# Gate and up by seven half-size products on TensorE, the gated product kept in DRAM, and the down product as a phase of its own

## The chip, the cores and the metric

The kernel runs on one core of one Trainium2 chip (trn2). The metric is the device time of one execution in microseconds; lower is better. All data are 32-bit floats in DRAM. The program is written in Bass and Tile: the program text gives operations and tiles, and a planner puts the instructions of each engine in a fixed order before the launch.

## The reference, cut to what matters

```python
SEQ, D_MODEL, D_FF, DEPTH = 512, 2048, 5632, 1
h = x                                              # 512 x 2048
xn = rms_norm(h, attn_norm_w)
...                                                # attention, convolution and recurrence groups
h = h + mix @ w_out
xn = rms_norm(h, ffn_norm_w)
ff = jax.nn.silu(xn @ w_gate) * (xn @ w_up)        # two products 512 x 2048 x 5632
h = h + ff @ w_down                                # 512 x 5632 x 2048
return rms_norm(h, final_norm_w)                   # y * rsqrt(mean(y*y) + 1e-6) * w
```

## The kernel before, in words

Activations lie transposed: a tile has 128 features on the partitions and the 512 tokens along the free axis, so `h` is 16 tiles of 128x512 and the gated product 44. Each float32 operand is split into a high part, rounded to float32r by a ScalarE copy, and a low part, the difference, by a VectorE subtraction (`split`, lines 130 to 138). A product of two such operands is three matmuls, high by high, high by low, low by high (`mm3`, lines 140 to 144). The weight is always the stationary operand (128x128), the activations the moving one.

Weights come from DRAM in half-blocks of 128x1024 (512 KB), each eight 128x128 stationary tiles. `weights` (lines 124 to 128) loads one through SyncE's DMA queue and splits it. It has two buffers for the loaded block (`raw`) and three each for the two parts (`wh`, `wl`). It runs under `high_priority(offset=6000)`: where the planner has several instructions of an engine that are ready, these come before all that stand up to 6000 places earlier in the program. The planner may also move matmuls past one another.

`cols_tile` (lines 146 to 155) makes one output tile of 128x512 in one PSUM bank: for a contraction of 16 tiles that is two half-blocks and, at three per contraction tile, 48 matmuls. `project` (660 to 675) makes `h` from `w_out`: per tile it loads `x`, adds the bank, splits `h * ffn_norm_w` into `hh` and `hl`, and adds up squares (ScalarE squares, GpSimd sums). `project_end` (677 to 680) makes `rstd`.

`ff_tile` (683 to 692) makes one of the 44 tiles of the gated product: 48 matmuls for gate, 48 for up, all 128 columns by 512 tokens; VectorE multiplies both banks by `rstd`, ScalarE applies silu, GpSimd multiplies the two, and the result is split for the next product. `ffn` (763 to 770) interleaves this with `down`: after each four tiles, `down` (694 to 701) adds their part of the down product to all 16 tiles of `h` in SBUF. The last four tiles go through `down_last` (703 to 757), which works by halves of the tokens (matmuls of 128x256), adds up the squares of the final `h`, and then makes the final norm and the output.

`run` (772 to 840) opens and closes the areas of SBUF and PSUM. Tiles of a new area may lie where tiles of a closed one lay; then their first writer waits for the last reader of what lay there. The gated product stays in SBUF, in the area `mix`.

Of the kernel before, what the change touches and what calls it, by code (L numbers as in the profile page):

```python
# [15 lines left out]
P = 128  # L16
# [11 lines left out]
GF = 4  # L28
NCHUNK = NF // GF
NB = S // P  # L30
# [41 lines left out]
class Area:  # L72
    """A pool whose tiles are named by a tag with its own number of buffers."""

# [15 lines left out]
class Trunk:  # L90
# [26 lines left out]

    # ---- weights: one half-block is [128, 1024] float32
    def weight_tiles(self):
# [19 lines left out]

    def mm3(self, out, a, b, first, last):  # L140
        mm = self.nc.tensor.matmul
        mm(out, a[0], b[0], start=first, stop=False)  # L142
        mm(out, a[0], b[1], start=False, stop=False)  # L143
        mm(out, a[1], b[0], start=False, stop=last)  # L144
# [70 lines left out]

    # ---- constants
    def consts(self):
# [103 lines left out]

    # ---- HGRN2, one head
    def hgrn_head(self, r2, w, hd):
# [106 lines left out]

    # ---- Conformer convolution
    def conv_tile(self, r1, gbank, abank, i):
# [36 lines left out]

    # ---- latents  # L470
    def latent(self, w, area, tag):
# [36 lines left out]

    # ---- attention
    def attention(self, w, r3):  # L510
# [147 lines left out]

    # ---- output projection and residual
    def project(self, w, r4):  # L660
        nc = self.nc
        self.hw = []
        sq_sum = self.sq_sum = r4("acc")
        for m in range(KT):
            nc.sync.dma_start(self.h[:, m], self.io["x"][m])
            bank = self.cols_tile(w, self.mix_y + self.mix)
            nc.vector.tensor_tensor(self.h[:, m], self.h[:, m], bank, op=ALU.add)
            self.hw.append(self.split(self.h[:, m], self.hp("hh", F32R), self.hp("hl", F32R),
                                      self.col("ffn_w", m)))
            if m == 0:  # L670
                nc.scalar.activation(sq_sum, self.h[:, m], AF.Square)
            else:
                q = r4("sq")
                nc.scalar.activation(q, self.h[:, m], AF.Square)
                nc.gpsimd.tensor_tensor(sq_sum, sq_sum, q, op=ALU.add)

    def project_end(self, r4):
        t = [r4(i) for i in ("sq", "sq", "acc")]
        r = self.rsqrt(self.sum_over_partitions(self.sq_sum), D, "eps", *t)
        self.nc.gpsimd.tensor_copy(self.rstd, r)  # L680

    # ---- feed-forward
    def ff_tile(self, w, r5):
        nc = self.nc
        gbank = self.cols_tile(w, self.hw)
        ubank = self.cols_tile(w, self.hw)
        g, u = r5("g"), r5("u")
        nc.vector.tensor_tensor(g, gbank, self.rstd, op=ALU.mult)  # L688
        self.last_silu = nc.scalar.activation(g, g, AF.Silu)
        nc.vector.tensor_tensor(u, ubank, self.rstd, op=ALU.mult)  # L690
        nc.gpsimd.tensor_tensor(u, u, g, op=ALU.mult)  # L691
        return self.split(u, self.mx("mx", F32R), self.mx("mx", F32R))

    def down(self, w, ff):
        nc = self.nc
        for m2 in range(KT // 2):
            h, l = self.weights(next(w))
            for i in range(2):
                m = 2 * m2 + i
                bank = self.four_tile(h, l, 4 * i, ff)  # L700
                nc.vector.tensor_tensor(self.h[:, m], self.h[:, m], bank, op=ALU.add)  # L701

    def down_last(self, w, ff, r5):
        """The last part of the product, the final norm and the output, by halves of the tokens."""
        nc = self.nc
        self.tables_after(self.last_silu)
        wt = []
        for m2 in range(KT // 2):
# [3 lines left out]
            else:  # L712
                raw = self.wp.tile([P, 1024], F32, tag="raw", name="raw", bufs=2)
                nc.sync.dma_start(raw, next(w))
                for s in (slice(0, S), slice(S, 2 * S)):
                    wt.append(self.split(raw[:, s], self.hp("hh", F32R), self.hp("hl", F32R)))
        n = S // 2
        acc = r5("acc")
        for th in range(2):
# [16 lines left out]
            for m in POOL_OUT:  # L736
                scaled[m] = o = self.mx("mx")
# [5 lines left out]
            r = self.rsqrt(bank, D, "eps", r5("g")[:, :n], r5("u")[:, :n], r5("sq", F32, (P, n)))  # L743
            for m in range(0, KT, 2):
                if m in scaled:
# [5 lines left out]
                    continue  # L751
                o = self.mx("mx")
                for i in range(2):
# [3 lines left out]
                self.put_out(m, ts, o)  # L757

    def put_out(self, m, ts, o):
# [3 lines left out]
    def ffn(self, wg, wd, r5):  # L763
        ff = [self.ff_tile(wg, r5) for _ in range(GF)]
        for c in range(NCHUNK - 1):
            nxt = [self.ff_tile(wg, r5)]
            self.down(wd, ff)
            nxt += [self.ff_tile(wg, r5) for _ in range(GF - 1)]
            ff = nxt
        self.down_last(wd, ff, r5)  # L770

    def run(self):
# [54 lines left out]
        ckvn.close()  # L827
        self.hp = area("hw", {"hh": KT, "hl": KT})
        late = area("late", {"h": 1}, "right")
        self.h = late("h", F32, (P, KT, S))  # L830
# [3 lines left out]
        self.ps = area("banks3", {"mm": 6, "ax": 2}, space=PSUM)  # L834
        self.project_end(r4)
        r4.close()
        r5 = area("ffn", {"g": 1, "u": 1, "sq": 3, "acc": 1}, "right")
        self.ffn(stream("w_gu"), stream("w_down"), r5)
        for a in (r5, late, self.hp, self.mx, self.ps):
# [21 lines left out]
def _arrange(inp):  # L861
# [36 lines left out]
    dn = a["w_down"][0]  # L898
    out["w_down"] = c(np.concatenate([_blocks_cols(dn[i * GF * P:(i + 1) * GF * P]) for i in range(NCHUNK)]))

# [54 lines left out]
```

## Time and profile before

| what | value |
|---|---|
| timed runs | 2212.8 us median of 3 (2211.44 to 2213.72) |
| profiled execution, first to last instruction (span) | 2210.9 us |
| TensorE matmul (PE) busy | 2175.6 us, 98% |
| TensorE weight load (PEld) busy | 1805.6 us, 82% |
| VectorE (DVE) busy | 1085.3 us, 49% |
| ScalarE (ACT) busy | 713.0 us, 32% |
| GpSimd (POOL) busy | 234.6 us, 11% |
| DMA | 220.52 MB, mean 100 GB/s |
| output projection, the matmuls after attention | up to 754.7 us of the span |
| gate, up and down, 512 tokens a matmul | 754.7 to 2148.1 us |
| last part of down, final norm, output | 2148.1 to 2210.9 us |

The only time that the profile gives for the execution is its span; the median of the timed runs is 1.9 us above it. Matmuls are pipelined: a record is longer than the distance to the next, so a rate is read as a stretch of time over the matmuls that began in it. "PEld" is the load of the stationary operand, which runs beside matmuls.

### The profile page before, as it was taken

To read this page: it belongs to the slowest core of one execution; us is meant where nothing else is said; L and a number is where in the kernel's file an instruction comes from. 1 tells how busy PE (TensorE), PEld (TensorE's weight loads), DVE (VectorE), ACT (ScalarE), POOL (GpSimd) and SP (SyncE) were. 2 spreads that over 40 slices of the span, in tenths; PEclk is the share of its full clock that TensorE was granted. 3 is DMA by queue.
4 is the path that set the end of the run, shared out by engine and by line. 5 is a ranking of instruction groups with operands and counts; after the bars stand their busy time and mean duration, and the time that the engine had idled before them with its cause. 6 is when DMAs were issued, how large, how long until landed. Compare 5 with 4: busy or idle time off the path is not lost.

```text
span 2210.9 us, 24879 instructions
## 1 busy us (share of the span) xinstructions
PE 2175.6 (98%) x10036; PEld 1805.6 (82%) x10036; DVE 1085.3 (49%) x1368; ACT 713.0 (32%) x1081; POOL 234.6 (11%) x195
## 2 busy tenths in 40 slices
PE   7999999999999999999999999999999999999997
PEld 6888788788778888888888888888888888888887
DVE  8896685557443334334343443434344343433437
ACT  6324664457432322222222222222222222222223
POOL 4102573100011100000000000000000000000001
PEclk9999999999999999999999999999999999999999
DMA  6233422313153333332323333333333332332332
GB/s 184 90 118 98 138 86 82 102 58 92 38 181 95 96 95 96 100 100 96 96 95 96 100 93 104 96 95 96 98 102 96 95 95 95 97 103 92 100 103 98
DMA packets 72595, 220.52 MB, mean 100 GB/s; under 512 B 7504, under 2 KB 15952, under 8 KB 72480
## 3 DMA queue, kind: packets, MB, share of 16 engines
q1 hardware_dynamic: 70192, 216.47, 31.4%
q10 hardware_dynamic: 2176, 2.10, 0.3%
q8 instruction: 79, 1.29, 0.2%
q0 software_dynamic: 112, 0.36, 0.0%
q14 instruction: 36, 0.29, 0.0%
HBM read 210.51 MB, written 8.39 MB: 99 GB/s over the span
## 4 chain that ended last, share of the span: by engine, by line
PE 94%; DVE 1%; ACT 1%; DMA 1%; POOL 1%; issue 1%; SPq 0%; DVEq 0%; ACTq 0%
PE mm L142 29%; PE mm L144 29%; PE mm L143 29%; PE lv L371 1%; PE ob L608 1%; PE lv L144 1%; PE lv L143 1%; PE lv L142 1%; DMA xraw<-in_x 1%; PE sc L583 0%; PE sc L584 0%; PE tb L600 0%; POOL ps L361 0%; DVE wl L134 0%; DMA raw<-in_w_down 0%
## 5 line engine op out<-in xcount | busy, mean ns | idle before, releaser
L133 ACT CAST wh<-raw 128x1024 fp32r<-128x1024 f32 (+1 forms) x379 | 391.3, 1034 | 1240.8 <-PE mm L143 1082.0
L134 DVE TENSOR_TENSOR wl<-raw,wh 128x1024 fp32r<-128x1024 f32 (+1 forms) x379 | 514.2, 1358 | 452.9 <-ACT wh L133 452.7
L142 PE MATMUL mm<-hh,wh 128*128 128x512 f32 x1408 | 548.1, 389 | 0.0
L144 PE MATMUL mm<-hh,wl 128*128 128x512 f32 x1408 | 547.7, 389 | 0.0
L143 PE MATMUL mm<-hl,wh 128*128 128x512 f32 x1408 | 547.7, 389 | 0.0
L142 PE MATMUL mm<-mx,wh 128*128 128x512 f32 (+1 forms) x944 | 361.4, 384 | 2.2 <-ACT mx L136 1.6
L144 PE MATMUL mm<-mx,wl 128*128 128x512 f32 (+1 forms) x944 | 362.3, 384 | 0.3 <-DVE wl L134 0.3
L143 PE MATMUL mm<-mx,wh 128*128 128x512 f32 (+1 forms) x944 | 362.3, 384 | 0.0
L143 PEld LDWEIGHTS mm<-hl,wh 128*128 128x128 f32 x1408 | 264.4, 188 | 55.1 <-issue 0.2
L142 PEld LDWEIGHTS mm<-hh,wh 128*128 128x128 f32 x1408 | 264.3, 188 | 55.0 <-issue 0.2
L144 PEld LDWEIGHTS mm<-hh,wl 128*128 128x128 f32 x1408 | 264.4, 188 | 54.8
L142 PEld LDWEIGHTS mm<-mx,wh 128*128 128x128 f32 x944 | 177.0, 188 | 37.6 <-ACT mx L136 2.0
L144 PEld LDWEIGHTS mm<-mx,wl 128*128 128x128 f32 x944 | 177.4, 188 | 35.8 <-DVE wl L134 1.2
L701 DVE TENSOR_TENSOR h<-h,mm 128x512 f32<-128x512 f32 x160 | 109.9, 687 | 196.9 <-PE mm L144 196.9
L143 PEld LDWEIGHTS mm<-mx,wh 128*128 128x128 f32 x944 | 177.4, 188 | 35.3 <-DVE mx L137 0.5
L691 POOL TENSOR_TENSOR u<-u,g 128x512 f32<-128x512 f32 x44 | 56.4, 1281 | 1327.5 <-ACT wh L133 1286.5
L142 PE MATMUL mm<-xh,wh 128*128 128x512 f32 x400 | 160.4, 401 | 6.8 <-ACT wh L133 6.8
L143 PE MATMUL mm<-xl,wh 128*128 128x512 f32 x400 | 158.6, 397 | 0.5 <-DVE xl L137 0.5
L144 PE MATMUL mm<-xh,wl 128*128 128x512 f32 x400 | 156.8, 395 | 0.0
L690 DVE TENSOR_TENSOR u<-mm,rstd 128x512 f32<-128x512 f32 x44 | 30.5, 692 | 145.5 <-PE mm L144 145.5
L688 DVE TENSOR_TENSOR g<-mm,rstd 128x512 f32<-128x512 f32 x44 | 30.4, 692 | 144.2 <-PE mm L144 144.2
L142 PEld LDWEIGHTS mm<-xh,wh 128*128 128x128 f32 x400 | 76.2, 191 | 23.6 <-ACT wh L133 6.0
(288 smaller groups left out, 1940.1 us busy)
## 6 DMA issues: line engine op xcount, KB each, us to landing
raw<-in_w_gu SPq DMA_DIRECT2D x176, 512.0 KB, 3.5
raw<-in_w_down SPq DMA_DIRECT2D x88, 512.0 KB, 3.5
raw<-in_w_cols SPq DMA_DIRECT2D x42, 512.0 KB, 3.5
raw<-in_w_out SPq DMA_DIRECT2D x32, 512.0 KB, 3.5
raw<-in_w_rows SPq DMA_DIRECT2D x16, 512.0 KB, 3.5
raw<-in_w_attn SPq DMA_DIRECT2D x14, 512.0 KB, 3.4
xraw<-in_x SPq DMA_DIRECT2D x16, 256.0 KB, 3.3
raw<-in_w_first SPq DMA_DIRECT2D x16, 256.0 KB, 3.2
```

What stands on the lines that cost most here:

```text
L133: nc.scalar.copy(h, src)
L134: nc.vector.tensor_tensor(l, src, h.bitcast(F32), op=ALU.subtract)
L142: mm(out, a[0], b[0], start=first, stop=False)
L143: mm(out, a[0], b[1], start=False, stop=False)
L144: mm(out, a[1], b[0], start=False, stop=last)
L371: nc.tensor.matmul(bank[:, c * 64:(c + 1) * 64], e[:, c * P:(c + 1) * P], ap_of(e, c * P + h, [2 * h, 64 // h], [1, h]), start=True, stop= ...
L608: nc.tensor.matmul(obank[:, qs], pt[:, js], vt[h // 4, j][:, hs], start=j == 0, stop=j == i)
L688: nc.vector.tensor_tensor(g, gbank, self.rstd, op=ALU.mult)
L690: nc.vector.tensor_tensor(u, ubank, self.rstd, op=ALU.mult)
L691: nc.gpsimd.tensor_tensor(u, u, g, op=ALU.mult)
L701: nc.vector.tensor_tensor(self.h[:, m], self.h[:, m], bank, op=ALU.add)
```

## The change

Gate and up are taken together, for 42 of the 44 tiles, as a product of a 2x2 block matrix of weights (the two halves of the contraction by gate and up) with a 2x2 block matrix of activations (the two halves of the contraction by the two halves of the tokens), in the form of Strassen and Winograd: seven products of half size, each 8 contraction tiles by 256 tokens, in place of eight. Two tiles (`PLAIN`) are made as before. The activations are not multiplied by `rstd` first; `h * ffn_norm_w` is kept as a float32 tile `hf`, from which `token_sums` makes the four sums of blocks that the algorithm needs, in two parts each. The sums of weight blocks are made per tile, in place in the loaded blocks.

The gated product is stored in a DRAM tile `ffd`, one tile of 256 KB each, and `h` in `hd`. A down phase of its own follows: it loads eight tiles of the gated product at a time through ScalarE's queue, splits them, and makes five passes over the 16 tiles of `h` with 24 matmuls each (128x512), then `down_last` with four tiles as before. The up branch is no longer multiplied by `rstd`; in place of that `h` is multiplied by `rms` (one over `rstd`) and the final norm's epsilon is scaled to match. Comments and docstrings were taken out. `mm3` passes a further keyword on to its matmuls.

```diff
+CF = 8
+NCHUNK = NF // CF
+PLAIN = 2
+HALF = 256
...
     def project(self, w, r4):
+            t = self.hf[:, m]
+            nc.sync.dma_start(t, self.io["x"][m])
             bank = self.cols_tile(w, self.mix_y + self.mix)
+            nc.vector.tensor_tensor(t, t, bank, op=ALU.add)
+            nc.scalar.dma_start(self.hd[m], t)
+            self.hw.append(self.split(t, self.hp("hh", F32R), self.hp("hl", F32R), self.col("ffn_w", m)))
...
+            nc.scalar.activation(t, t, AF.Copy, scale=self.col("ffn_w", m))
...
+    def token_sums(self, sp, tp):
+        n = KT // 2
+        H = {i: (sp("sh", F32R, (P, n, HALF)), sp("sl", F32R, (P, n, HALF))) for i in (1, 2, 3, 4)}
+        for j in range(0, n, 4):
+            q = lambda k, t: self.hf[:, k * n + j:k * n + j + 4, t * HALF:(t + 1) * HALF]
+            def parts(t, i):
+                self.split(t, *(x[:, j:j + 4] for x in H[i]))
+            s1 = tp("s", F32, (P, 4, HALF))
+            tt(s1, q(0, 1), q(1, 1), op=ALU.add)
+            parts(s1, 1)
+            tt(q(0, 1), q(0, 0), q(0, 1), op=ALU.subtract)
+            tt(s1, s1, q(0, 0), op=ALU.subtract)
+            parts(s1, 2)
+            parts(q(0, 1), 3)
+            tt(q(1, 0), q(1, 0), s1, op=ALU.subtract)
+            parts(q(1, 0), 4)
...
+    def put_ff(self, f, g, u):
+        nc.vector.tensor_tensor(g, g, self.rstd, op=ALU.mult)
+        self.last_silu = nc.scalar.activation(g, g, AF.Silu)
+        nc.vector.tensor_tensor(u, u, g, op=ALU.mult)
+        nc.sync.dma_start(self.ffd[f], u)
...
+    def ff_fast(self, f, w, rp, fp):
+        with self.tc.high_priority(offset=6000):
+            b11, b21, b12, b22 = raws = [rp("raw", F32, W) for _ in range(4)]
+            for t in raws:
+                nc.sync.dma_start(t, next(w))
...
+        product(one, early(parts, b11), "11")
+        nc.scalar.copy(pa, one[:, lo])
+        product(two, early(parts, b21), "12")
+        tt(g[:, lo], pa, two[:, lo], op=ALU.add)
+        def sums():
+            tt(b11, b12, b11, op=ALU.subtract)
+            t2 = rp("t2", F32, W)
+            tt(t2, b22, b11, op=ALU.subtract)
+            tt(b21, t2, b21, op=ALU.subtract)
+            return t2
+        t2 = early(sums)
+        product(one, early(parts, t2), "S2", start=False)
+        nc.scalar.copy(pb, one[:, lo])
+        product(three, early(parts, b11), "S1")
+        early(lambda: tt(b12, b22, b12, op=ALU.subtract))
+        product(one, early(parts, b12), "S3", start=False)
+        nc.scalar.copy(pc, one[:, lo])
+        tt(u[:, hi], pc, three[:, lo], op=ALU.add)
+        product(four, early(parts, b21), "22")
+        tt(g[:, hi], pc, four[:, lo], op=ALU.subtract)
+        product(three, early(parts, b22), "S4", start=False)
+        tt(u[:, lo], pb, three[:, lo], op=ALU.add)
+        self.put_ff(f, g, u)
...
+    def ff_load(self, k, fp):
+        with self.tc.high_priority(offset=3000):
+            t = fp("fr")
+            nc.scalar.dma_start(t, self.ffd[k])
+            return self.split(t, fp("fh", F32R), fp("fl", F32R))
     def down(self, w, ff):
+        for m in range(KT):
+            bank = self.cols_tile(w, ff)
+            nc.vector.tensor_tensor(self.h[:, m], self.h[:, m], bank, op=ALU.add)
...
+    def down_all(self, w, fp, r5, lp):
+        ff = [self.ff_load(k, fp) for k in range(CF)]
+        for m in range(KT):
+            nc.scalar.dma_start(self.h[:, m], self.hd[m])
+            nc.vector.tensor_tensor(self.h[:, m], self.h[:, m], self.rms, op=ALU.mult)
+        for c in range(NCHUNK):
+            at = (c + 1) * CF
+            nxt = [self.ff_load(k, fp) for k in range(at, min(at + CF, NF))]
+            self.down(w, ff)
+            ff = nxt
+        self.down_last(w, ff, r5, lp)
...
+        for f in range(PLAIN):
+            self.ff_plain(f, wg, fp)
+        rp = area("raw4", {"raw": 5, "t2": 1}, "right")
+        for f in range(PLAIN, NF):
+            self.ff_fast(f, wg, rp, fp)
...
+        fp = area("ff", {"fr": 3, "fh": 2 * CF, "fl": 2 * CF})
+        lp = area("last", {"wlh": 10, "wll": 10, "mx": 8}, "right")
```

In `ff_fast`, `product` issues 8 contraction tiles by three matmuls of 128x256 into one bank, `parts` splits a block of 128x1024 into `wh` and `wl`, and `early` runs its argument under `high_priority(offset=6000)`. `one` to `four` are four of eight PSUM banks, and `pa`, `pb`, `pc` are 128x256 copies of a bank in SBUF, two buffers each. The area of the sums lies where `mix` lay; `raw4` and the tiles of `ff_fast` lie where `hf` lay; the area `ff` lies where the sums lay, and `h` of the down phase where `hh` lay. The blocks of `w_down` are laid out for chunks of eight tiles.

## Rows read from the trace of the kernel before

**Rows 1.** the page: span, busy time of the engines, the chain that ended last

```profile
span 2210.9 us, 24879 instructions
...
PE 2175.6 (98%) x10036; PEld 1805.6 (82%) x10036; DVE 1085.3 (49%) x1368; ACT 713.0 (32%) x1081; POOL 234.6 (11%) x195
...
PE 94%; DVE 1%; ACT 1%; DMA 1%; POOL 1%; issue 1%; SPq 0%; DVEq 0%; ACTq 0%
```

**Rows 2.** windows: length, busy time (instructions) by engine, clock, DMA

```profile
core 0: us, PE busy (x) PEld busy (x) DVE busy (x) ACT busy (x) POOL busy (x), PEclk, DMA share, GB/s
608.00:613.00 5.00, 3.44 (x13) 1.95 (x12) 2.47 (x3) 3.28 (x5) 0.00 (x0) 1.00 0.63 174
754.70:2148.10 1393.40, 1393.40 (x6147) 1153.80 (x6146) 559.21 (x551) 325.72 (x350) 57.46 (x45) 1.00 0.31 97
2148.10:2158.00 9.90, 9.31 (x77) 9.09 (x76) 7.06 (x10) 4.34 (x8) 1.30 (x1) 1.00 0.34 106
2165.00:2195.00 30.00, 30.00 (x251) 29.95 (x250) 25.02 (x63) 12.51 (x32) 3.42 (x4) 1.00 0.21 71
```

**Rows 3.** groups by form, TensorE: count, busy us, mean ns, idle

```profile
L142 PE MATMUL mm<-hh,wh 128*128 128x512 f32 x1408 | 548.1, 389 | 0.0
...
L142 PE MATMUL mm<-mx,hh 128*128 128x256 f32 x80 | 22.7, 284 | 0.6 <-DVE h L728 0.6
...
L143 PEld LDWEIGHTS mm<-mx,hh 128*128 128x128 f32 x80 | 15.4, 192 | 0.0
```

**Rows 4.** timeline of ScalarE and VectorE in the projection: start, duration

```profile
689.32 1.05 ACT L133 CAST wh<-raw 128x1024 fp32r<-128x1024 f32 x1 [4.39 <-PE mm L143]
690.28 0.72 ACT L136 ACTIVATE hh<-h,cols 128x512 fp32r<-128x512 f32 x1
...
689.50 0.69 DVE L667 TENSOR_TENSOR h<-h,mm 128x512 f32<-128x512 f32 x1 [3.31 <-PE mm L144]
690.41 1.23 DVE L134 TENSOR_TENSOR wl<-raw,wh 128x1024 fp32r<-128x1024 f32 x1 [0.22 <-ACT wh L133]
691.55 0.75 DVE L137 SCALAR_TENSOR_TENSOR hl<-h,cols,hh 128x512 fp32r<-128x512 f32 x1
```

**Rows 5.** groups of VectorE, ScalarE, GpSimd, by form

```profile
L688 DVE TENSOR_TENSOR g<-mm,rstd 128x512 f32<-128x512 f32 x44 | 30.4, 692 | 144.2 <-PE mm L144 144.2
...
L728 DVE TENSOR_TENSOR h<-h,mm 128x256 f32<-128x256 f32 x32 | 12.8, 417 | 2.8 <-PE mm L144 2.6
...
L689 ACT ACTIVATE g<-g 128x512 f32<-128x512 f32 x44 | 27.7, 629 | 0.6 <-DVE g L688 0.6
...
L589 ACT ACTIVATE p<-sc,nmx 128x256 f32<-128x256 f32 x8 | 3.8, 473 | 6.7 <-DVE nmx L587 6.6
...
L691 POOL TENSOR_TENSOR u<-u,g 128x512 f32<-128x512 f32 x44 | 56.4, 1281 | 1327.5 <-ACT wh L133 1286.5
```

**Rows 6.** timeline of TensorE where the last head's result comes in

```profile
603.72 0.96 PE L142 MATMUL mm<-mx,wh 128*128 128x512 f32 x3 [0.83 <-ACT mx L136]
604.51 0.49 PE L143 MATMUL mm<-mx,wh 128*128 128x512 f32 x1
```

**Rows 7.** timeline of VectorE from the last tile of the projection to rstd

```profile
754.78 0.69 DVE L667 TENSOR_TENSOR h<-h,mm 128x512 f32<-128x512 f32 x1 [3.31 <-PE mm L144]
...
765.29 0.69 DVE L185 SCALAR_TENSOR_TENSOR sq<-acc,sq 128x512 f32<-128x512 f32 x1
```

**Rows 8.** DMA issues: transfer, queue, count, KB each, median us to landing

```profile
raw<-in_w_gu SPq DMA_DIRECT2D x176, 512.0 KB, 3.5
...
yr<-yd SPq DMA_DIRECT2D x8, 256.0 KB, 2.9
...
vh<-vd SPq DMA_DIRECT2D x4, 256.0 KB, 5.2
...
yd<-og SPq DMA_DIRECT2D x4, 256.0 KB, 4.1
```

**Rows 9.** chain of waits near the end: start, us, what

```profile
2197.83 0.48 ACT u L180
```

More of the change, by code (lines that the diff above doesn't have):

```diff
@@ L138, in split, with mm3 @@
         return h, l
-    def mm3(self, out, a, b, first, last):
+    def mm3(self, out, a, b, first, last, **k):
         mm = self.nc.tensor.matmul
-        mm(out, a[0], b[0], start=first, stop=False)
-        mm(out, a[0], b[1], start=False, stop=False)
-        mm(out, a[1], b[0], start=False, stop=last)
+        mm(out, a[0], b[0], start=first, stop=False, **k)
+        mm(out, a[0], b[1], start=False, stop=False, **k)
+        mm(out, a[1], b[0], start=False, stop=last, **k)
     def cols_tile(self, w, rhs):
@@ new lines, in project_end @@
+        nc.vector.tensor_tensor(self.rms, self.rms, r, op=ALU.mult)
+        nc.vector.tensor_copy(self.rstd, r)
+    def token_sums(self, sp, tp):
+        nc = self.nc
+        n = KT // 2
+        tt = nc.vector.tensor_tensor
+        H = {i: (sp("sh", F32R, (P, n, HALF)), sp("sl", F32R, (P, n, HALF))) for i in (1, 2, 3, 4)}
[12 more added lines that the diff above has]
+            parts(q(1, 0), 4)
+        raw = lambda k, t: [tuple(x[:, t * HALF:(t + 1) * HALF] for x in self.hw[k * n + i]) for i in range(n)]
+        form = lambda hl: [(hl[0][:, i], hl[1][:, i]) for i in range(n)]
+        self.A = {"11": raw(0, 0), "12": raw(1, 0), "22": raw(1, 1),
+                  **{f"S{i}": form(H[i]) for i in H}}
@@ new lines, in ff_fast, with parts, product, early @@
+    def ff_fast(self, f, w, rp, fp):
+        nc = self.nc
+        tt = nc.vector.tensor_tensor
+        W = (P, 1024)
+        with self.tc.high_priority(offset=6000):
+            b11, b21, b12, b22 = raws = [rp("raw", F32, W) for _ in range(4)]
+            for t in raws:
+                nc.sync.dma_start(t, next(w))
+        def parts(t):
+            h, l = (self.wp.tile([P, 1024], F32R, tag=x, name=x) for x in ("wh", "wl"))
+            return self.split(t, h, l)
+        def product(bank, hl, a, start=True):
+            h, l = hl
+            n = KT // 2
+            for p in range(n):
+                s = slice(p * P, (p + 1) * P)
+                self.mm3(bank[:, :HALF], (h[:, s], l[:, s]), self.A[a][p], start and p == 0, p == n - 1,
+                         skip_group_check=not start)
+        def early(f, *a):
+            with self.tc.high_priority(offset=6000):
+                return f(*a)
+        one, two, three, four = (self.ps("mm") for _ in range(4))
+        lo, hi = slice(0, HALF), slice(HALF, S)
+        g, u = fp("g"), fp("u")
+        pa, pb, pc = fp("pa", F32, (P, HALF)), fp("pb", F32, (P, HALF)), fp("pc", F32, (P, HALF))
+        product(one, early(parts, b11), "11")
[21 more added lines that the diff above has]
+        self.put_ff(f, g, u)
@@ L694, in down @@
+    def ff_load(self, k, fp):
+        nc = self.nc
+        with self.tc.high_priority(offset=3000):
+            t = fp("fr")
+            nc.scalar.dma_start(t, self.ffd[k])
+            return self.split(t, fp("fh", F32R), fp("fl", F32R))
     def down(self, w, ff):
         nc = self.nc
[L696 to L701, printed above, removed]
@@ L715, in down_last @@
                 for s in (slice(0, S), slice(S, 2 * S)):
-                    wt.append(self.split(raw[:, s], self.hp("hh", F32R), self.hp("hl", F32R)))
+                    wt.append(self.split(raw[:, s], lp("wlh", F32R), lp("wll", F32R)))
         n = S // 2
@@ L757, in down_last, with rsqrt_of @@
                 self.put_out(m, ts, o)
+    def rsqrt_of(self, total, epsv, v, y, q):
+        nc = self.nc
+        nc.vector.scalar_tensor_tensor(v, total, 1.0 / D, epsv, ALU.mult, ALU.add)
+        self.after(nc.scalar.activation(y, v, AF.Ln), self.tables)
+        nc.scalar.activation(y, y, AF.Exp, scale=-0.5)
+        nc.scalar.activation(q, y, AF.Square)
+        nc.vector.scalar_tensor_tensor(q, q, -0.5, v, ALU.mult, ALU.mult)
+        nc.vector.scalar_tensor_tensor(v, q, 1.5, y, ALU.add, ALU.mult)
+        return v
     def put_out(self, m, ts, o):
@@ L827, in run @@
         ckvn.close()
[L828 to L830 removed]
+        stat = area("stat", {"rms": 1, "epsv": 1}, "right")
+        self.rms, self.epsv = stat("rms"), stat("epsv")
+        self.hp = area("hw", {"hh": KT, "hl": KT}, "right")
+        whole = area("whole", {"hf": 1}, "right")
+        self.hf = whole("hf", F32, (P, KT, S))
         r4 = area("rest", {"acc": 1, "sq": 2}, "right")
@@ L833, in run @@
         self.ps.close()
-        self.ps = area("banks3", {"mm": 6, "ax": 2}, space=PSUM)
+        self.ps = area("banks3", {"mm": 8}, space=PSUM)
         self.project_end(r4)
         r4.close()
-        r5 = area("ffn", {"g": 1, "u": 1, "sq": 3, "acc": 1}, "right")
-        self.ffn(stream("w_gu"), stream("w_down"), r5)
-        for a in (r5, late, self.hp, self.mx, self.ps):
+        self.mx.close()
+        sp = area("sums", {"sh": 4, "sl": 4})
+        tp = area("sum", {"s": 1}, "right")
+        self.ffd = self.dp.tile([NF, P, S], F32, name="ffd")
+        wg = stream("w_gu")
+        self.token_sums(sp, tp)
+        tp.close()
+        whole.close()
+        fp = area("gu", {"g": 2, "u": 2, "pa": 2, "pb": 2, "pc": 2}, "right")
+        for f in range(PLAIN):
[3 more added lines that the diff above has]
+            self.ff_fast(f, wg, rp, fp)
+        rp.close()
+        fp.close()
+        self.hp.close()
+        sp.close()
+        self.ps.close()
+        self.ps = area("banks4", {"mm": 6, "ax": 2}, space=PSUM)
+        late = area("late", {"h": 1}, "right")
+        self.h = late("h", F32, (P, KT, S))
+        fp = area("ff", {"fr": 3, "fh": 2 * CF, "fl": 2 * CF})
+        lp = area("last", {"wlh": 10, "wll": 10, "mx": 8}, "right")
+        r5 = area("ffn", {"v": 1, "y": 1, "sq": 3, "acc": 1}, "right")
+        self.down_all(stream("w_down"), fp, r5, lp)
+        for a in (r5, lp, fp, late, stat, self.ps):
             a.close()
@@ L898, in _arrange @@
     dn = a["w_down"][0]
-    out["w_down"] = c(np.concatenate([_blocks_cols(dn[i * GF * P:(i + 1) * GF * P]) for i in range(NCHUNK)]))
+    parts = [_blocks_cols(dn[i * CF * P:(i + 1) * CF * P]) for i in range(NCHUNK)]
+    out["w_down"] = c(np.concatenate(parts + [_blocks_cols(dn[NCHUNK * CF * P:])]))
     cols = np.zeros((P, NCOL), np.float32)
```

45 lines of the change are left out of this document (19 added, 26 removed).

## The prediction

> **What bounds the kernel now.** I read the page's busy times and chain first. TensorE is busy 98% of 2210.9 us, and 94% of the chain that ended last is TensorE [rows 1]. Next the table of windows, by stage. From 754.7 to 2148.1 us, the whole of gate, up and down at 512 tokens, TensorE is busy for 1393.40 of 1393.40 us at clock 1.00, while VectorE is at 559.21/1393.4 = 40% and ScalarE at 23% [rows 2]. So only fewer or cheaper matmuls help there, and nothing else costs anything as long as it stays hidden. The groups by form serve for single durations. A matmul's record (389 ns for 512 columns) overlaps the next one's, so the price of one is the window over its count: 1393.40/6147 = 0.2267 us for 512 columns and 30.00/250 = 0.120 us for 256, the latter from the window in which the kernel already works by token halves [rows 2, 3]. Twice 0.120 is 0.0133 more than 0.2267: each matmul carries a fixed 13 ns, and Strassen pays it more often.
>
> **The matmuls.** A tile of the gated product has 2 x 16 x 3 = 96 matmuls of 512 columns: 96 x 0.2267 = 21.76 us. By Strassen it has 7 x 8 x 3 = 168 of 256 columns: 168 x 0.120 = 20.16 us. That is 1.60 us less (7%, not an eighth), and for 42 tiles 67.2 us. With 251 matmuls in the 30 us, 0.1195 us, it would be 70.6. The down product keeps its count: 40 x 16 x 3 = 1920 of 512 columns, then 384 of 256.
>
> The rows put the fixed part at 13 ns a matmul. [...]
>
> **The loop beside the matmuls.** VectorE per tile: seven splits and four sums of weight blocks, eleven operations of 128x1024 at 1.23 us, or 1.14 from start to start (690.41 to 691.55) [rows 4], 12.5 to 13.5 us; four 128x256 operations that read a bank at 0.42, 1.7 us; two of 128x512 at 0.69, 1.4 us (one of them replaces GpSimd's 1.28) [rows 5]. Together 15.6 to 16.6 of 20.16 us, about 80% against 40% now. ScalarE: 7 x 1.05 for the splits, three copies from a bank at 0.47 (the nearest row: an activation of 128x256 from a bank), silu 0.63: 9.4 us, 47% [rows 4, 5]. DMA: 2.1 MB of weights and a 0.26 MB store in 20.16 us are 117 GB/s; the trace shows 174 GB/s at a share of 0.63 [rows 2]. A store waits on SyncE's queue for its `u`, some 3 us after the tile's last product; loads behind it wait too, but with five `raw` buffers these are due products later. By sums TensorE stays the bound; what is open is the order.
>
> The tight place is the seventh product. It accumulates into bank `three`, out of which the second token half of `u` must first be read: end of the fifth product, ScalarE's copy `pc` (0.47), VectorE's addition (0.42). Its cover is the sixth product, 24 x 0.120 = 2.88 us. With both queues empty the wait costs nothing: record end 0.16 after the next start, 0.16 + 0.47 + 0.42 = 1.05. But the next tile's splits and sums are traced at high priority and become ready in the same stretch: a split on ScalarE (1.05), then up to six operations on VectorE at 1.14, so the addition ends at 0.16 + 1.05 + 6.84 + 0.42 = 8.5, and the seventh product comes 5.6 us late. TensorE need not stand still meanwhile: the planner moves matmuls past others that wait, as where three high-part matmuls go ahead together behind a wait of 0.83 us [rows 6], and the next tile's first two products, 5.76 us, have their weights split by then. So the cost lies between 0 and 5.6 us a tile. I take 0.3: the nearest row is that wait of 0.83, met at about one tile in three. 42 x 0.3 = 12.6 us; own range 0 to 0.8 a tile, 0 to 34 us.
>
> **Into the loop.** `project` gains per tile a store (256 KB, ScalarE's queue) and a scaled copy in place (0.72), in 10.9 us of TensorE time that leave ScalarE mostly idle: nothing, since two plain tiles (2 x 21.76 = 43.5 us) cover what comes after. `token_sums` is 16 VectorE operations of 1.23 us, 19.7 us, and 8 ScalarE copies for its splits. Its `s` lies where the scratch of `project_end` lay, so it starts after that chain's last step, at 765.3 + 0.7, 11 us after TensorE's last projection matmul at 754.7 [rows 7], and shares VectorE with six splits and an eviction pair (about 8 us): done some 11 + 20 + 8 = 39 us in. The blocks of the first fast tile lie where `hf` lay, so their loads start only then: 3.5 us for the first [rows 8], a split of 2.3 us, 45 us against 43.5. The fourth block comes later (2.1 MB at 174/0.63 = 276 GB/s is 7.6 us), and the third product needs it through two sums and a split. I take 3 us, range 0 to 10.
>
> **Into down.** The first load of `ffd` needs the space of the first sums, read last in the fourth product of the last tile, 8.6 us before the end. Eight tiles through three buffers are three rounds of a load (2.9 us) and a split (0.62 + 0.69): about 13 us, 8.6 covered, and TensorE can begin with the first tiles. `h` follows on the same queue, 16 loads of 256 KB and a multiplication of 0.69 each; the first is due one block (5.4 us) later, with six banks of slack. I take 3 us. If a load had to wait for the last store of the DRAM tile instead, it would be `u` (0.42 + 0.69 + 0.63 + 0.69), a store of up to 4.1, a load of up to 5.2 and 1.3 for the split: 13 us [rows 5, 8]. Range 0 to 13. Afterwards a block of 5.44 us holds one split, one addition and half a split of `ffd` on VectorE (2.6 us) and 0.64 MB (118 GB/s): hidden.
>
> **The end.** The window at 2148.1 holds 77 matmuls where 9.9/0.120 = 82 fit: 0.6 us lost to late weights, which now have tiles of their own: -0.6 [rows 2]. In the last norm the logarithm now waits for a VectorE step of about 0.48, which ran beside it: +0.5 [rows 9].
>
> **Sum.** -67.2 + 12.6 + 3 + 3 - 0.6 + 0.5 = -48.7: the span becomes 2162.2 us. The median of the runs is 1.9 above the span, so 2164 us.
>
> **The rivals.**
> *Order on VectorE (slower).* The seventh product's wait is not filled: the planner's order leaves TensorE standing behind the addition to `u`. It decides from (67.2 - 6)/42 = 1.46 us a tile. Half the price, 2.8 us, gives 2212.8 + 6 + 42 x (2.8 - 1.6) = 2269 us; the whole, 5.6, 2387. For it: VectorE at 80% and six operations of higher priority in one gap. Against: VectorE's queue still has 3.5 us free in each tile, and matmuls are seen to be moved. Chance 0.18.
> *No change.* Waits of 1.36 to 1.56 us a tile eat the gain: 2208 to 2217 us. For it: a thin margin of 1.6; against: nothing singles that size out. Chance 0.05.
> *The fixed 13 ns goes.* If a long row of 256-column matmuls paid none of it, a tile would take 168 x (0.120 - 0.0133) = 17.9 us, 2.2 less than forecast: 2164 - 42 x 2.2 = 2070 us. Against: 250 loads in 30.00 us without a gap [rows 2]. Chance 0.02. [...]
> *Weight loads bind (it does not do what it says).* A load's record is 192 ns, longer than 120 [rows 3]. Were loads not overlapped, a tile would take 168 x 0.192 = 32.3 us, the run 2212.8 + 42 x 10.5 = 2654. Against: the same window, where loads of 192 ns start every 120. Chance 0.01.
>
> **Numbers.** The likeliest case has 0.74 and, with pitch 0.1195 and no waits, 2142 us at the low end; with 34, 10 and 13 us for the three places, 2202 at the high end. A measurement of this kernel tells about 0.2%, 4.4 us, from no change. Faster 0.74 + 0.02 = 0.76, same 0.05, slower 0.18 + 0.01 = 0.19. Reaching up through the case of no change, 2142 to 2217 leaves 0.2 out.
>
> **What would show it.** Right: in a window in the middle of the loop TensorE near 100% busy with 8.3 matmuls per us, VectorE near 80%; groups of 128x256 matmuls with 7056 in sum; small gaps at the loop's two ends. Wrong: idle time of TensorE that ends on VectorE's additions or on `wl`, over 1.46 us a tile; a gap of over 10 us before the down product; a loop at the old clock but with fewer than 8 matmuls per us while busy.

## The result, and the profile after

The kernel after takes 2165.2 us (median of 4 runs, 2163.1 to 2166.1) against 2213.1 before on the same chip (2211.4 to 2213.7): a ratio of 0.978 with a 95% interval of 0.977 to 0.980. Forecast were 2164 us. The agreement is partly luck: the price of the matmuls, the waits in the loop and the ways in and out were all off, in opposite directions.

The page of the profile after, against [rows 1]:

```profile
span 2163.8 us, 31928 instructions
...
PE 2111.9 (98%) x13060; PEld 1894.6 (88%) x13060; DVE 1391.6 (64%) x1786; ACT 893.8 (41%) x1357; POOL 171.3 (8%) x150
...
PE 92%; DVE 2%; DMA 2%; ACT 2%; POOL 1%; issue 1%; SPq 0%; DVEq 0%; ACTq 0%; POOLq 0%
```

The windows after, with the columns of [rows 2]: the way into the gated product, the middle of the loop of fast tiles, the way out of it (two rows), a long stretch of the down phase, and the last part of down.

```profile
756.00:765.00 9.00, 5.18 (x14) 3.65 (x15) 5.07 (x7) 4.64 (x7) 1.38 (x1) 0.81 0.27 89
...
1200.00:1640.00 440.00, 440.00 (x3699) 440.00 (x3698) 336.36 (x375) 188.93 (x242) 0.00 (x0) 1.00 0.37 115
1640.00:1665.00 25.00, 15.26 (x81) 13.07 (x80) 16.98 (x26) 7.81 (x10) 0.00 (x0) 0.80 0.84 304
1665.00:1690.00 25.00, 21.60 (x79) 16.05 (x78) 15.91 (x23) 11.05 (x16) 0.00 (x0) 0.86 0.62 191
1690.00:2080.00 390.00, 390.00 (x1722) 322.95 (x1721) 153.75 (x172) 92.09 (x100) 0.00 (x0) 1.00 0.35 115
2104.00:2151.00 47.00, 44.43 (x368) 43.56 (x366) 36.42 (x86) 21.65 (x52) 3.40 (x4) 0.99 0.29 91
```

In the middle of the loop TensorE is busy for 440.00 of 440.00 us, with 8.4 matmuls per us (8.3 forecast), and VectorE for 76% (80% forecast). In the whole loop TensorE is never idle. The losses stand at its two ends: 5.18 us busy of 9 on the way in, 15.26 of 25 on the way out, both at a lower granted clock: 0.81 and 0.80 over these windows, and 0.50 in parts of them (761 to 763 us, 1652 to 1660 us).

The timeline of TensorE shows the two ends (start, duration, and in brackets the idle time before and what ended it); three rows of ScalarE's queue and a cast show what stood ahead of the second, and the row at 1646.23 is the loop's last matmul.

```profile
759.82 1.52 PE L197 MATMUL mm<-acc,ones 128*128 128x512 f32 x2 [3.95 <-POOL acc L681]
...
1643.29 1.29 ACTq L887 DMA_DIRECT2D h<-hd  x3
...
1646.23 0.28 PE L147 MATMUL mm<-sh,wl 128*128 128x256 f32 x1
...
1646.65 1.71 ACTq L802 DMA_DIRECT2D fr<-ffd  x3
...
1650.00 5.51 ACTq L887 DMA_DIRECT2D h<-hd  x6
1655.56 0.62 ACT L136 CAST fh<-fr 128x512 fp32r<-128x512 f32 x1 [7.87 <-DMA h<-hd]
...
1656.22 1.65 PE L145 MATMUL mm<-fh,wh 128*128 128x512 f32 x3 [9.72 <-ACT fh L136]
...
1678.76 0.79 PE L145 MATMUL mm<-fh,wh 128*128 128x512 f32 x1 [2.92 <-ACT wh L136]
```

Where the 47.1 us of span went (2210.9 to 2163.8):

| stretch | how read | us |
|---|---|---|
| loop of 42 fast tiles | a tile every 19.99 us (the addition `u<-pc,mm` starts 42 times from 823.2 to 1642.9) for 21.76: 42 x 1.77 | -74.4 |
| way out of the loop and down | 1646.35 to 2101.40 is 455.05; 1920 x 0.2267 is 435.3 | +19.8 |
| last part, final norm, output | 62.4 for 62.8 | -0.4 |
| projection's end and way into the loop | the remainder; 1.0 of it is that the projection's matmuls end at 755.7 for 754.7 | +7.9 |

### The profile page after: what moved, and what is told of

Same layout as the page of the kernel before. It is cut to its first block, busy times and chain, and to the rows that moved or that the text cites. A ratio compares the mean times of both kernels' runs of the same rounds, so it can differ in the third digit from the quotient of the medians.

```text
span 2163.8 us, 31928 instructions
## 1 busy us (share of the span) xinstructions
PE 2111.9 (98%) x13060; PEld 1894.6 (88%) x13060; DVE 1391.6 (64%) x1786; ACT 893.8 (41%) x1357; POOL 171.3 (8%) x150
## 4 chain that ended last, share of the span: by engine, by line
PE 92%; DVE 2%; DMA 2%; ACT 2%; POOL 1%; issue 1%; SPq 0%; DVEq 0%; ACTq 0%; POOLq 0%
PE mm L145 28%; PE mm L147 28%; PE mm L146 28%; PE lv L374 1%; PE ob L611 1%; PE lv L147 1%; PE lv L145 1%; PE lv L146 1%; DVE mx L862 1%; PE sc L586 1%; PE sc L587 1%; DMA xraw<-in_x 0%; DMA fr<-ffd 0%; PE tb L603 0%; ACT wh L136 0%
## 5 line engine op out<-in xcount | busy, mean ns | idle before, releaser
L146 PE MATMUL mm<-sl,wh 128*128 128x256 f32 x1344 | 378.3, 283 | 0.0
L145 PE MATMUL mm<-sh,wh 128*128 128x256 f32 x1344 | 378.1, 283 | 0.0
L147 PE MATMUL mm<-sh,wl 128*128 128x256 f32 x1344 | 373.5, 283 | 0.0
L145 PE MATMUL mm<-hh,wh 128*128 128x256 f32 (+1 forms) x1072 | 307.9, 287 | 0.0
L147 PE MATMUL mm<-hh,wl 128*128 128x256 f32 (+1 forms) x1072 | 307.5, 287 | 0.0
L146 PE MATMUL mm<-hl,wh 128*128 128x256 f32 (+1 forms) x1072 | 307.1, 286 | 0.0
L145 PE MATMUL mm<-fh,wh 128*128 128x512 f32 (+1 forms) x688 | 263.3, 386 | 12.9 <-ACT fh L136 9.7
L146 PE MATMUL mm<-fl,wh 128*128 128x512 f32 (+1 forms) x688 | 264.5, 385 | 0.2 <-DVE fl L137 0.2
L147 PE MATMUL mm<-fh,wl 128*128 128x512 f32 (+1 forms) x688 | 264.0, 384 | 0.0
L146 PEld LDWEIGHTS mm<-sl,wh 128*128 128x128 f32 x1344 | 257.5, 192 | 0.0
```

Source lines behind the costliest of these rows:

```text
L145: mm(out, a[0], b[0], start=first, stop=False, **k)
L146: mm(out, a[0], b[1], start=False, stop=False, **k)
L147: mm(out, a[1], b[0], start=False, stop=last, **k)
```

## Experiments

All were timed beside runs of the kernel before, whose medians lay between 2212.6 and 2214.3; they ran on different chips, so a difference between two versions is good to about 2 us. Except where said, each starts from the kernel after.

**The sum over partitions in a bank of its own.** The first wait is that of a matmul with ones, which sums squares over the partitions. Its bank comes from the tag that the gate matmuls use, and it stands ahead of them on TensorE's queue.

```diff
-        total = self.sum_over_partitions(self.sq_sum, "mm")
+        total = self.sum_over_partitions(self.sq_sum)
...
-        self.ps = area("banks3", {"mm": 8}, space=PSUM)
+        self.ps = area("banks3", {"mm": 7, "ax": 1}, space=PSUM)
```

> The sum over partitions for rstd gets a bank of its own tag, as before the change (seven banks for products, one for it); the planner then sets it behind some 30 matmuls of the first plain tile. My theory: the changed kernel loses about 8 us at the loop's entry because TensorE stands 3.95 us behind the sum of squares and then works at half clock until 763.7 us; here no wait and no low clock between the projection and the first plain tile, and 2165 - 6 = 2159 us (2156 to 2162). Rival: the entry's cost is only moved, since the token sums start as late and the first fast tile waits for its blocks instead: the gap turns up at about 800 us and the time stays at 2165.

Measured: 2159.6 us (2156.1 to 2160.8), ratio 0.976 (0.975 to 0.978). The window that had 5.18 us busy, the matmul with ones, and a wait that this run has in its first fast tile:

```profile
756.00:765.00 9.00, 9.00 (x39) 7.08 (x38) 4.50 (x6) 3.93 (x6) 0.35 (x1) 1.00 0.30 110
```

```profile
759.60 1.02 PE L197 MATMUL ax<-acc,ones 128*128 128x512 f32 x2
...
804.13 0.39 PE L147 MATMUL mm<-sh,wl 128*128 128x256 f32 x1 [0.88 <-DVE wl L137]
```

The matmul with ones now stands behind some 20 gate matmuls and waits for nothing. The wait and the lower clock are gone, and with them 5.6 us. So the way in was not lost to late weight blocks, as forecast, but to the order on TensorE's queue. Only with this wait gone do the blocks of the first fast tile come late, by 0.88 us; that much of the rival holds.

**`h` behind the first tiles of the gated product.** Six loads of `h` stand on ScalarE's queue ahead of the first load of `ffd`, and six more ahead of the first cast.

```diff
-            nc.scalar.dma_start(t, self.ffd[k])
+            self.last_fr = nc.scalar.dma_start(t, self.ffd[k])
...
-            nc.scalar.dma_start(self.h[:, m], self.hd[m])
+            self.after(nc.scalar.dma_start(self.h[:, m], self.hd[m]), self.last_fr)
```

> The 16 loads of h for the down phase are held on ScalarE's queue behind the first eight loads of the gated product. My theory: TensorE's 9.7 us gap before down is the first gated tiles queueing behind six loads of h and two blocks of w_down at 304 GB/s; with h behind, the first tile lands about 3.6 us after its issue, the gap falls to 4 to 5 us, the clock falls less, and the time is 2165 - 6 = 2159 us (2155 to 2162). Rival 1: the gap comes from ScalarE's order (the issue stands behind a weight cast that waits for w_down) and stays near 9 us: 2164 to 2166. Rival 2: h comes so late that the first additions wait and TensorE runs out of banks: a gap of over 5 us near the second or third block, 2165 or more.

Measured: 2154.9 us (2153.7 to 2155.8), ratio 0.974 (0.973 to 0.975). The wait ahead of down on TensorE:

```profile
1651.73 1.65 PE L145 MATMUL mm<-fh,wh 128*128 128x512 f32 x3 [5.39 <-ACT fh L136]
```

9.72 us became 5.39, the second wait 0.53 with a later one of 1.35, and the run is 10.3 us shorter: about half of the exit was the queue.

**No loads of `h`.** `h` is zeroed by GpSimd instead; the residual is left out.

```diff
-            nc.scalar.dma_start(self.h[:, m], self.hd[m])
+            nc.gpsimd.memset(self.h[:, m], 0.0)
```

> Leaves out the 16 loads of h for the down phase (h is set to zero by GpSimd, so the residual is missing from the output). It sizes what these loads cost at the loop's end. My theory: gap before down of 3 to 5 us in place of 9.7, and no second gap; 2165 - 8 = 2157 us (2153 to 2160). Rival (the order on ScalarE alone): gap of 8 us or more, 2163 to 2166. This is the floor for any order of these loads.

Measured: 2155.9 us (one run). TensorE's waits (what it waited for, sum, times, longest):

```profile
PE mm L145 <- ACT fh L136: 4.7, 1, 4.7
PE mm L146 <- DVE fl L137: 4.2, 1, 4.2
```

Without any load of `h` the run is no shorter than with `h` behind, so a wait for something else is left. The 4.2 us behind VectorE belong to this run alone: GpSimd zeroes `h` between 1640 and 1650 us (16 operations, 7.52 us), so the 16 multiplications of `h` by `rms` can come early. VectorE is busy for 9.89 of these 10 us and for 8.03 of the next 10; that the multiplications stand there ahead of the split that TensorE waits for is argued from the order, not shown apart. What the rest is, this run doesn't settle; the one with the last tile plain does.

**All 44 tiles plain.** The rest of the change stays: DRAM tile, phase of its own for down.

```diff
-PLAIN = 2
+PLAIN = NF
```

> All 44 tiles of the gated product are made as before the change (PLAIN = 44); the DRAM trip, the phases and the token sums stay (their results are not used). It prices the split into phases by itself. My theory: the loop by Strassen saves 42 x (21.76 - 19.98) = 74.9 us, and the ends cost about 27 us: 2165.2 + 74.9 = 2240 us (2235 to 2245), slower than before the change by 27 us. Rival: the ends are nearly free (as predicted, 6 us) and the loop saved only 48 to 54 us: 2213 to 2219.

Measured: 2230.6 us (2227.3 to 2231.1), ratio 1.008 (1.006 to 1.009). A window in its gate and up, TensorE's waits from the way in to the last part of down, and the loads of `ffd` (durations in ns, first and last start):

```profile
800.00:1700.00 900.00, 900.00 (x3934) 738.40 (x3933) 267.70 (x262) 204.17 (x221) 0.00 (x0) 1.00 0.35 114
```

```profile
PE mm L197 <- POOL acc L681: 4.0, 1, 4.0
PE mm L145 <- DVE u L737: 0.9, 1, 0.9
```

```profile
L802 ACTq DMA_DIRECT2D fr<-ffd x44: 326/327/1157, 799.5 to 2077.6; - x44
```

The seven products are thus worth 65 us net, and the rest of the change costs 18 (2230.6 against 2212.6 before). This run's exit waits 0.9 us only: nothing reads the sums there, so their space is free early, and the first load of `ffd` goes out at 799.5 us. And 900.00/3934 is 0.2288 us a matmul, where the kernel before has 0.2267 [rows 2]; the last experiment takes that up. A plain tile so takes 21.96 us here, and the loop of 42 fast ones is 42 x (21.96 - 19.99) = 83 us shorter; some 17 of them go again at the exit of the kernel after. The two also explain the expectation, which was 10 us too high: some 19 less at the exit, 42 x 0.2 = 8 more in the tiles.

**The last tile plain.** If it is the space of the sums that the loads of `ffd` wait for, it can be freed one tile earlier.

```diff
-        for f in range(PLAIN, NF):
+        for f in range(PLAIN, NF - 1):
             self.ff_fast(f, wg, rp, fp)
         rp.close()
+        sp.close()
+        ffp = area("ff", {"fr": 3, "fh": 2 * CF, "fl": 2 * CF})
+        first = [self.ff_load(k, ffp) for k in range(CF)]
+        self.ff_plain(NF - 1, wg, fp)
...
-        sp.close()
...
-        fp = area("ff", {"fr": 3, "fh": 2 * CF, "fl": 2 * CF})
+        fp = ffp
```

> The last of the 44 tiles is made as two plain products; the areas of the sums and of the weight blocks are closed before it, and the first eight tiles of the gated product are loaded for the down phase from then on. Theory (space: the loads of the down phase wait until the space of the sums is free, and 48 weight matmuls' time more would hide them): the waits of 9.72 and 2.92 us at the start of down and most of their half clock go, about 15 of the 19.8 us that this place costs, and the tile costs 21.96 - 19.98 = 2.0 us more: 2165.2 - 15 + 2 = 2152 us. Rival (the loads wait for the tile's own stores, or for their queue, not for space): the wait stays, 2165 + 2 = 2167 us.

Measured: 2146.9 us (2146.0 to 2149.3), ratio 0.970 (0.969 to 0.972). The first loads on ScalarE's queue, and the window of the down phase:

```profile
1630.54 0.81 ACTq L802 DMA_DIRECT2D fr<-ffd  x2
```

```profile
1640.00:2080.00 440.00, 440.00 (x1942) 364.16 (x1941) 188.96 (x219) 111.04 (x123) 0.00 (x0) 1.00 0.39 130
```

TensorE does not wait any more, at clock 1.00. The first loads again go out as the last fast tile's last matmul ends, here a plain tile before the down phase. They are then ahead of those of `h` on the queue too, so this edit removes the queue's part together with the space's. The exit's 19.8 us go and the plain tile costs 2.0: 2165.2 - 17.8 = 2147.4, as measured. I had expected the lower clock (0.50 in the kernel after, 1652 to 1660 us) to stay in part; without a wait it reads 1.00 from 1640 to 2080 us.

**VectorE with two and with four operations more in each tile.** They compare a weight block with itself, at the splits' priority. The first added line is in the run with four only.

```diff
         tt(u[:, hi], pc, three[:, lo], op=ALU.add)
+        early(lambda: [tt(b21, b21, b21, op=ALU.max) for _ in range(2)])
         product(four, early(parts, b21), "22")
         tt(g[:, hi], pc, four[:, lo], op=ALU.subtract)
+        early(lambda: [tt(b22, b22, b22, op=ALU.max) for _ in range(2)])
```

> Each fast tile gets two more VectorE operations of 128x1024 at the splits' priority (a block compared with itself, which leaves its values), 2 x 1.14 to 1.23 us. In the kernel after, VectorE is busy for 336.36 of 440.00 us, 15.3 of 19.98 us a tile; here 17.6 to 17.8, 88 to 89%. Theory: what counts is VectorE's rate, and the planner hides the order: TensorE stays at 100% busy in the middle of the loop, the run at 2165 us within 4. Rival (order): the second half of the gated product's tile is read later by up to 2.4 us a tile, which the sixth product's cover (1.8 us) no longer holds: waits of 0.6 to 2.4 us a tile, 2190 to 2265 us.

> Four more such operations a tile, 4 x 1.14 to 1.23 us: VectorE at 19.9 to 20.2 us a tile against 19.98 of TensorE. Theory (rate): the margin is just used up; VectorE over 98% busy in the middle of the loop, TensorE just under 100%, the run between 2165 and 2180 us. Rival (order): waits as in the run with two, doubled, 1.2 to 4.8 us a tile: 2215 to 2367 us.

Measured: 2185.0 us with two, 2194.5 with four (one run each). The middle of the loop with two, and the row of the one wait in each tile with the split that it is for and the matmuls next to it:

```profile
1200.00:1640.00 440.00, 434.95 (x3609) 430.48 (x3609) 374.16 (x407) 184.42 (x236) 0.00 (x0) 1.00 0.37 118
```

```profile
1300.54 1.22 DVE L793 TENSOR_TENSOR raw<-raw 128x1024 f32<-128x1024 f32 x1
1301.68 1.22 DVE L137 TENSOR_TENSOR wl<-t,wh 128x1024 fp32r<-128x1024 f32 x1
...
1302.44 0.28 PE L146 MATMUL mm<-sl,wh 128*128 128x256 f32 x1
1302.95 0.39 PE L147 MATMUL mm<-sh,wl 128*128 128x256 f32 x1 [0.23 <-DVE wl L137]
1303.17 0.28 PE L145 MATMUL mm<-sh,wh 128*128 128x256 f32 x1
```

And with four, with the one wait in each tile:

```profile
1200.00:1640.00 440.00, 432.18 (x3555) 424.57 (x3553) 415.41 (x445) 178.42 (x232) 0.00 (x0) 1.00 0.37 114
```

```profile
1298.77 0.38 PE L147 MATMUL mm<-hh,wl 128*128 128x256 f32 x1 [0.35 <-DVE wl L137]
```

Neither theory holds. VectorE is at 85% with two, so its rate is not used up, yet each tile takes 20.48 us for 19.99 and 42 x 0.49 = 20 us are lost; the rival's place, the seventh product, has no wait. The place is the third product, which waits for the split of `t2`. With four a tile takes 20.79 us, VectorE is at 94%, and the wait is at another product, one on `hh`, for another split. In the kernel after, in the middle of the loop (the first matmul behind the fifth product, an addition to `u` before and after one tile, the first matmul of the seventh product and the first behind it, the split of `t2`, the first matmul of the third product that reads this split):

```profile
1300.72 0.28 PE L147 MATMUL mm<-hh,wl 128*128 128x256 f32 x1
...
1303.02 0.41 DVE L790 TENSOR_TENSOR u<-pc,mm 128x256 f32<-128x256 f32 x1
...
1305.91 0.28 PE L145 MATMUL mm<-sh,wh 128*128 128x256 f32 x1
...
1308.78 0.28 PE L146 MATMUL mm<-hl,wh 128*128 128x256 f32 x1
...
1310.30 1.22 DVE L137 TENSOR_TENSOR wl<-t,wh 128x1024 fp32r<-128x1024 f32 x1
...
1312.32 0.28 PE L147 MATMUL mm<-sh,wl 128*128 128x256 f32 x1
...
1323.02 0.41 DVE L790 TENSOR_TENSOR u<-pc,mm 128x256 f32<-128x256 f32 x1
```

The split ends at 1311.52 and is read at 1312.32: a margin of 0.80 us. One operation of 1.14 us ahead of it (L793 at 1300.54 above) is more than that by 0.34. The trace of the run with two shows what makes 0.49 of it: the matmul that waits starts 0.51 us behind the one before it, where 0.12 is usual, and the next one 0.22 behind that.

The seventh product has 1305.91 - 1303.43 = 2.5 us. It owes most of them to the planner: between the fifth product and the seventh stand 44 matmuls on `hh`, 5.19 us, and a product has 24. So besides the sixth most of the next tile's first product is there. The last fast tile has no next one, and there the cover is used up (the addition, the last matmul of the sixth product, the first of the seventh):

```profile
1642.91 0.41 DVE L790 TENSOR_TENSOR u<-pc,mm 128x256 f32<-128x256 f32 x1
1643.08 0.28 PE L147 MATMUL mm<-hh,wl 128*128 128x256 f32 x1
1643.38 0.38 PE L145 MATMUL mm<-sh,wh 128*128 128x256 f32 x1
```

The seventh product starts 0.30 us behind the sixth's last matmul, where 0.12 is usual, just after the addition ends at 1643.32.

**The order that the first rival feared.** The second half of `u` is read behind the next tile's third sum.

```diff
-            tt(b21, t2, b21, op=ALU.subtract)
+            s = tt(b21, t2, b21, op=ALU.subtract)
+            if f > PLAIN:
+                self.after(self.late, s)
...
-        tt(u[:, hi], pc, three[:, lo], op=ALU.add)
+        late = tt(u[:, hi], pc, three[:, lo], op=ALU.add)
...
+        self.late = late
```

> The addition that reads the second token half of `u` out of bank `three` is ordered on VectorE behind the next tile's third sum: the order that the first rival of the prediction feared, in each of the 41 following tiles. Rival as forecast: the seventh product stands and TensorE with it, 2.8 to 5.6 us a tile, 2165 + 41 x 2.8 to 5.6 = 2280 to 2395 us. Theory: the planner lets the next tile's first two products (2 x 2.86 us) go ahead of the seventh, TensorE stays over 97% busy in the middle of the loop, and the run is at 2165 to 2180 us.

Measured: 2205.2 us (one run). The middle of its loop, and the wait in each tile:

```profile
1200.00:1640.00 440.00, 422.46 (x3506) 418.15 (x3506) 325.71 (x357) 183.59 (x231) 0.00 (x0) 1.00 0.34 112
```

```profile
1312.81 1.04 ACT L136 CAST wh<-raw 128x1024 fp32r<-128x1024 f32 x1 [1.00 <-PE mm L146]
1313.47 0.42 DVE L792 TENSOR_TENSOR u<-pc,mm 128x256 f32<-128x256 f32 x1
...
1313.90 0.39 PE L145 MATMUL mm<-sh,wh 128*128 128x256 f32 x1 [0.83 <-ACT wh L136]
```

A tile takes 21.09 us, 1.10 more than in the kernel after, between the two expectations. TensorE does run three products on `hh` in a row here (about 1304.4 to 1312.6) where the kernel after has the seventh between them, so the planner does move matmuls; that this takes most of the 5.6 us off is argued from the order, not shown apart. The rest is a wait that the view puts on a cast ending at 1313.85; the late addition ends at 1313.89, and the trace can't tell the two apart. At 1.10 us a tile even this order would have stayed under the 1.46 from which the rival decides: the run is still faster than before.

**Both ends.** The last tile plain, and the sum over partitions in its own bank.

> The last tile plain with the loads of the down phase ahead of it, and the sum over partitions in a bank and a tag of its own. Theory (the two ends are separate costs and add up): the kernel with the last tile plain, 2146.9 us, less the 5.6 us that the bank alone brought (2165.2 - 2159.6): 2141.3 us; TensorE busy without a wait from 756 us to the start of the last part of down near 2075. Rival (the time comes back at the exit, where the loads then meet the same DMA earlier): 2147 us.

Measured: 2141.4 us (2139.5 to 2141.7, 5 runs), ratio 0.967 (0.966 to 0.968): the best version, 23.8 us below the kernel after. From the projection to the last part of down:

```profile
756.00:2070.00 1314.00, 1313.32 (x9061) 1227.38 (x9060) 855.33 (x956) 489.57 (x604) 1.41 (x1) 1.00 0.38 123
```

One wait is left, 0.68 us in the first fast tile, as in the run with the bank alone. The two ends are separate costs: 18.2 and 5.6 us add up.

**The kernel before, with `hh` and `hl` on the other side of SBUF.** Nothing else is changed, and this one starts from the kernel before. The program opens an area `left` (the default, as here before the edit) or `right`.

```diff
-        self.hp = area("hw", {"hh": KT, "hl": KT})
+        self.hp = area("hw", {"hh": KT, "hl": KT}, "right")
```

> The kernel before, with the area of `hh` and `hl` on the other side of SBUF, where the kernel after has it; nothing else. Theory (the place of the tiles sets the distance between matmuls: in the kernel after, plain tiles go at 0.2288 us a matmul of 512 columns, against 0.2267 before): 4224 matmuls x 2.1 ns = 8.9 us more, 2222 us, with 0.2288 us a matmul in gate and up. Rival (something else, such as what VectorE or the DMA do beside it): 2213 us, 0.2267.

Measured: 2222.3 us (2219.4 to 2223.8), ratio 1.0036 (1.0023 to 1.0050): slower by 0.4%. Gate, up and down, against the row of 6147 matmuls in [rows 2]; then a stretch of down alone and one of gate and up alone:

```profile
754.70:2148.10 1393.40, 1393.40 (x6103) 1146.22 (x6102) 556.72 (x549) 322.60 (x346) 57.95 (x45) 1.00 0.31 96
...
996.00:1038.00 42.00, 42.00 (x187) 34.76 (x186) 21.47 (x24) 8.01 (x8) 0.99 (x1) 1.00 0.33 100
1040.00:1125.00 85.00, 85.00 (x373) 69.75 (x373) 28.84 (x26) 19.82 (x22) 3.88 (x3) 1.00 0.32 95
```

The same two stretches of the kernel before:

```profile
996.00:1038.00 42.00, 42.00 (x187) 34.80 (x186) 21.66 (x24) 8.01 (x8) 1.17 (x1) 1.00 0.31 99
1040.00:1125.00 85.00, 85.00 (x377) 70.41 (x376) 28.96 (x26) 19.80 (x22) 3.84 (x3) 1.00 0.32 99
```

The edit also shifts what is laid out after the area, but only the matmuls that read `hh` and `hl` change: 373 of them where there were 377, while those of down, which read the gated product, keep their 187. Without a wait in either run, the other place of the moving operand so costs 44 x 0.228 = 10 us of TensorE's time from 754.70 to 2148.10. It goes the same way as the 0.2288 us of the run with all tiles plain, and by estimate (42 x 0.2, as above) accounts for 8 of the 18 us that that run lies above the kernel before. Why the place matters is open.

## Why the prediction was right, and where it was not

- *TensorE bounds, and only the matmuls' count and price matter.* Right: no wait in the loop, the down phase at its old price (390.00/1722 = 0.2265 us a matmul), VectorE 76%, ScalarE 43% (forecast 80 and 47), DMA 115 GB/s (117).
- *A tile's matmuls at 0.120 us, -67.2.* The mechanism is right, the size short by 7: 19.99/168 is 0.1190 us, and the loop gave 74.4. The distance of 0.120 came from a window in the last part of down. In the loop the products on the sums keep it (1305.91 to 1308.78 holds 24 matmuls, 0.120), those on `hh` have less (1300.72 to 1305.91 holds 44, 0.118). Why is open.
- *Waits in the loop, +12.6.* This step failed; they are 0. I priced a wait at the seventh product and met none: the addition to `u` is ordered ahead of the next tile's sums, and there are 2.5 us to spare. The forecast also counted on the sixth product's 2.88 us alone as cover, and the planner had put most of the next tile's first product there too. That was needed: the addition ends 2.71 us behind the fifth product (1303.43 - 1300.72), not 1.05, and in the last tile, without that help, the seventh product does start late, by 0.18 us. The tight place was one that the text did not name, the split of `t2` for the third product, with 0.80 us, and it held. With the order that I feared, the price is 1.10 us a tile, 45 us in the loop and 40 in the run.
- *Into the loop, +3.* The size is short (7.9, of which the projection, priced at nothing, has 1.0) and the mechanism wrong. The weight blocks were not late: TensorE has no wait at the first fast tile. The matmul with ones stood ahead of the gate matmuls and waited 3.95 us for GpSimd, and the clock was at 0.81 over the 9 us around it; its removal brought 5.6 us. The text followed the chain to `rstd` on VectorE and did not ask what it holds up on TensorE.
- *Into down, +3, range 0 to 13.* This step failed most: 19.8 us, outside its range. It is 13.1 us of waits (9.72, 2.92 and two of 0.2 to 0.3) and, by an estimate, 6.1 of the other 6.7 us is a lower clock in the stretches at 0.80 and 0.86 that they lie in: behind the two long waits the clock reads 0.50 and most 512-column matmuls stand 0.43 us apart (0.2267 before), 12 of them in 5.29 us from 1656.22 and 13 in 6.70 us from 1678.76, with a wait of 0.25, where 25 x 0.2267 is 5.67. The space of the sums was named, and so was the queue that `h` shares with the loads; that `h` goes ahead on that queue and that the clock falls were not in the sum. The 8.6 us of cover were not there either: the first load was to go out when the fourth product of the last tile had read its sums, and it goes out at 1646.65, behind the seventh (its last matmul starts at 1646.23). Freeing the space a tile earlier, with the loads ahead of `h`, removed all of it.
- *The end, -0.6 and +0.5.* Right within 0.3 us: -0.4 for -0.1.

So the total came out because the loop was 20 us better than forecast (7 by the price, 13 by waits that aren't there) and the two ends with the projection 21.7 us worse. The direction and the likeliest case were rightly read; the hit to 1 us was not earned.

## What to carry to other kernels

Where one engine is busy 100% of a stretch, price its work by the window over the count, and then look at the stretch's two ends first: here 23.8 us were lost there, matters of order and space that two small edits removed. Of a chain with one wait per iteration, ask for the margin of each product's operand, not for the busy share of the engine that makes it: VectorE at 85% already cost 20 us. A faster inner loop doesn't shorten what has to happen between two phases (19.8 us here); open the next phase's buffers one iteration early, which here, with the loads ahead of `h`, removed all of it for 2.0 us.

## What the runs showed of the hardware

- In the kernel before, 377 matmuls of 512 columns began or ran in 85.00 us with their moving operands `hh` and `hl` in an area on the left, and 373 with the area on the right, without a gap in either run; over gate, up and down together it is 0.2267 and 0.2283 us each. Beside them VectorE was busy for 28.96 and 28.84 of the 85.00 us, ScalarE for 19.80 and 19.82. For 256 columns, in the kernel after, the sign seems to be the other way (0.118 on `hh`, on the right, 0.120 on the sums, on the left), but there the operands differ too, and it wasn't tried apart.
- Around waits of 3.95 and 9.72 us the granted clock read 0.81 and 0.80, over 9 and 25 us, with parts of each at 0.50 (761 to 763 and 1652 to 1660 us). Where the waits went, so did that: 1.00 from 756 to 765 us with the sum in a bank of its own, and from 1640 to 1665 us with the last tile plain. The price of the waits was about one and a half times their length (19.8 us for 13.1, 5.6 for 3.95).
- While the way out moved 304 GB/s (1640 to 1665 us), loads of 256 KB on ScalarE's queue took from issue to landing the median in us at the end of each row; over the whole run those of `ffd` have a median of 3.6.

```profile
h<-hd ACTq DMA_DIRECT2D x16, 256.0 KB, 5.7
...
fr<-ffd ACTq DMA_DIRECT2D x6, 256.0 KB, 6.2
```
